# Linear attention with ReLU features: K and V with four heads on 128 partitions, a wider block-diagonal V, and the DMAs at both ends rearranged

## The chip, the cores and the metric

The kernel runs on one core of one Trainium2 chip. The metric is device time in microseconds (us). The profiler's span, from the first to the last instruction, is about 2 us shorter. PE is TensorE (matmuls), PEld its weight loads, DVE is VectorE, ACT is ScalarE, POOL is GpSimd, SP is SyncE. A name with a q (ACTq, SPq) is that engine's sequencer. "Granted clock" (PEclk) is the TensorE clock that the throttle let through, as a share of full speed.

## The reference

Eight batches of twelve heads, sequence 512, head size 64, all fp32:

```python
Q_feat = np.maximum(0, Q);  K_feat = np.maximum(0, K)          # [8, 12, 512, 64]
KV          = np.einsum('bhkd,bhkv->bhdv', K_feat, V)
K_sum       = np.sum(K_feat, axis=2)
numerator   = np.einsum('bhqd,bhdv->bhqv', Q_feat, KV)
denominator = np.einsum('bhqd,bhd->bhq', Q_feat, K_sum)
return numerator / (denominator[:, :, :, None] + 1e-10)
```

So 37.7 MB are read and 12.6 MB are written, with little arithmetic on them.

## The kernel before

The 96 heads are done in 24 groups of four. K and V of a group lie as two pairs: a pair's two heads fill 128 partitions, 64 each, so a row is 2 KB in fp32. GpSimd issues the loads and casts to bf16 on the way. V is spread into a block-diagonal tile (two heads, each with a column of ones for the K sum), so that one matmul serves two heads.

```python
def prep(g):
    kf[g] = kfp.tile([P, PR, R, 2, D], bf16, name="kf")
    nc.vector.tensor_scalar(kf[g]..., k_sb[g]..., scalar1=0.0, scalar2=None, op0=Alu.max)
    for h in range(2):                                   # V into the block diagonal, both on DVE
        hs = slice(64 * h, 64 * h + 64)
        nc.vector.tensor_copy(vbd[g % NB][hs, :, :, h, 0:D]..., v_sb[g][hs]...)

def mm_kv(g):                                            # 2 x 8 matmuls of 130 columns
    ...
def evac_kv(g):                                          # ACT, PSUM -> SBUF
    for t in range(2):
        nc.scalar.copy(kvd[...], ps_kv[g][...])
...                                                      # cut: transp, evac_qt, mm_out, norm

zero(0); prep(0)
for g in range(NG):
    mm_kv(g)
    evac_kv(g)
    if g + 1 < NG:
        ...                                              # cut: zero(g + 1) for the first groups
        prep(g + 1)
    if g > 0:
        mm_out(g - 1)
        store(g - 1, norm(g - 1))                        # SP; the last five wait for the last Q load
    transp(g)
    evac_qt(g)                                           # ACT
mm_out(NG - 1)
store(NG - 1, norm(NG - 1))
```

The order is the program's: every engine runs its share in the order in which it is written here.

Of the kernel before, what the change touches and what calls it, by code (L numbers as in the profile page):

```python
# [9 lines left out]
@with_exitstack  # L10
def kernel(
    ctx: ExitStack,
    tc: tile.TileContext,
    Q: bass.AP,
    K: bass.AP,
    V: bass.AP,
    out: bass.AP,
):
    nc = tc.nc
    B, H, S, D = Q.shape  # L20
    assert D == 64
    P = 128
    D1 = D + 1
    NH = B * H


    R = S * 2 // P
    RQ = S * 4 // P
    PR = 2
    NHG = 2 * PR  # L30
    U = RQ // 2
    NG = NH // NHG
    assert NG * NHG == NH and R == 8 and RQ == 16
    HOLD = 5

    fp32 = mybir.dt.float32
    bf16 = mybir.dt.bfloat16
    Act = mybir.ActivationFunctionType
    Alu = mybir.AluOpType

    def pool(name, bufs, **kw):
        return ctx.enter_context(tc.tile_pool(name=name, bufs=bufs, **kw))

    consts = pool("consts", 1)
    qin = pool("qin", NG)
    kin = pool("kin", 20)
    vin = pool("vin", 20)
    kfp = pool("kfp", 3)
    qtp = pool("qtp", 3)
    rcp = pool("rcp", 4)  # L50
    outp = pool("outp", 10)
    pkv = pool("pkv", 2, space=bass.MemoryType.PSUM)
    pqt = pool("pqt", 2, space=bass.MemoryType.PSUM)
    pou = pool("pou", 2, space=bass.MemoryType.PSUM)

    def rview(X):
        return X.rearrange("b h s d -> (b h s d)").rearrange(
            "(n j p f) -> n p j f", p=P, f=R * D, j=PR)

    def qview(X):  # L60
        return X.rearrange("b h s d -> (b h s d)").rearrange("(n p f) -> n p f", p=P, f=RQ * D)

    Qr, Kr, Vr, Or = qview(Q), rview(K), rview(V), qview(out)

    ident = consts.tile([P, P], bf16, name="ident")
    NB = 3



    vbf = [consts.tile([P, PR * R * 2 * D1], bf16, name=f"vbd{i}") for i in range(NB)]  # L70
    kvf = [consts.tile([P, PR * 2 * 2 * D1], bf16, name=f"kvd{i}") for i in range(NB)]
    vbd = [x.rearrange("p (j r h d) -> p j r h d", j=PR, r=R, h=2) for x in vbf]
    kvd = [x.rearrange("p (j h t d) -> p j h t d", j=PR, h=2, t=2) for x in kvf]

    ctx.enter_context(tc.manual_schedule())

    q_sb, k_sb, v_sb = {}, {}, {}
    last_q = {}

    def load(g):  # L80
        k_sb[g] = kin.tile([P, PR, R, D], bf16, name="k_sb")
        nc.gpsimd.dma_start(out=k_sb[g].rearrange("p j r d -> p j (r d)"), in_=Kr[g])  # L82
        v_sb[g] = vin.tile([P, PR, R, D], bf16, name="v_sb")
        nc.gpsimd.dma_start(out=v_sb[g].rearrange("p j r d -> p j (r d)"), in_=Vr[g])  # L84
        q_sb[g] = qin.tile([P, U, 2 * D], bf16, name="q_sb")
        last_q[g] = nc.gpsimd.dma_start(out=q_sb[g].rearrange("p u f -> p (u f)"), in_=Qr[g])  # L86

    load(0)
    make_identity(nc, ident)
    for g in range(1, NG):  # L90
        load(g)

    def zero(i):
        nc.vector.memset(vbf[i].bitcast(fp32), 0.0)  # L94
        for h in range(2):
            nc.vector.memset(vbd[i][64 * h:64 * h + 64, :, :, h, D:D1].rearrange("p j r o -> p (j r) o"), 1.0)  # L96
        nc.vector.memset(kvf[i].bitcast(fp32), 0.0)  # L97

    kf, qt, ps_kv, ps_qt, ps_out = {}, {}, {}, {}, {}

    def prep(g):
        kf[g] = kfp.tile([P, PR, R, 2, D], bf16, name="kf")
        nc.vector.tensor_scalar(  # L103
            kf[g].rearrange("p j r c d -> p (j r) c d"),
            k_sb[g].rearrange("p j r d -> p (j r) d").unsqueeze(2).to_broadcast([P, PR * R, 2, D]),
            scalar1=0.0, scalar2=None, op0=Alu.max)
        for h in range(2):
            hs = slice(64 * h, 64 * h + 64)
            nc.vector.tensor_copy(  # L109
                vbd[g % NB][hs, :, :, h, 0:D].rearrange("p j r d -> p (j r) d"),  # L110
                v_sb[g][hs].rearrange("p j r d -> p (j r) d"))

    def mm_kv(g):
        ps_kv[g] = pkv.tile([P, PR, 2, D1], fp32, name="ps_kv")
        for j in range(PR):
            for r in range(R):
                nc.tensor.matmul(  # L117
                    ps_kv[g][:, j, :, :],
                    kf[g][:, j, r, :, :].rearrange("p c d -> p (c d)"),
                    vbd[g % NB][:, j, r, :, :],  # L120
                    start=(r == 0), stop=(r == R - 1), skip_group_check=True)

    def evac_kv(g):
        for t in range(2):
            ts_ = slice(64 * t, 64 * t + 64)
            nc.scalar.copy(kvd[g % NB][ts_, :, :, t, :].rearrange("p j h d -> p (j h) d"),  # L126
                           ps_kv[g][ts_].rearrange("p j h d -> p (j h) d"))

    def transp(g):
        ps_qt[g] = pqt.tile([P, U, P], bf16, name="ps_qt")  # L130
        for u in range(U):
            nc.tensor.transpose(ps_qt[g][:, u, :], q_sb[g][:, u, :], ident)  # L132

    def evac_qt(g):
        qt[g] = qtp.tile([P, U, P], bf16, name="qt")
        nc.scalar.activation(  # L136
            qt[g].rearrange("p u q -> p (u q)"), ps_qt[g].rearrange("p u q -> p (u q)"), Act.Relu)

    def mm_out(g):
        for j in range(2):  # L140
            po = pou.tile([P, 2, 512], fp32, name="ps_out")
            ps_out[g, j] = po
            for v in range(U // 2):
                u = j * (U // 2) + v
                for h in range(NHG):
                    hs = slice(32 * h, 32 * h + 32)
                    nc.tensor.matmul(  # L147
                        po[hs, v // 2, (v % 2) * 2 * D1:(v % 2) * 2 * D1 + 2 * D1],
                        qt[g][:, u, hs],
                        kvd[g % NB][:, h // 2, h % 2, :, :],  # L150
                        start=True, stop=True, skip_group_check=True)

    def norm(g):
        o_sb = outp.tile([P, RQ, D], fp32, name="o_sb")
        for j in range(2):
            pv = ps_out[g, j][:, :, 0:4 * D1].rearrange("p b (r d) -> p b r d", d=D1)
            den = rcp.tile([P, 2, 4], fp32, name="den")
            nc.vector.tensor_scalar(den, pv[:, :, :, D], scalar1=1e-10, scalar2=None, op0=Alu.add)  # L158
            rec = rcp.tile([P, 2, 4], fp32, name="rec")
            nc.vector.reciprocal(rec, den)  # L160
            nc.vector.tensor_tensor(  # L161
                o_sb[:, 8 * j:8 * j + 8].rearrange("p (b r) d -> p b r d", b=2),
                pv[:, :, :, 0:D],
                rec.unsqueeze(3).to_broadcast([P, 2, 4, D]), op=Alu.mult)
        return o_sb

    def store(g, o_sb):
        st = nc.sync.dma_start(out=Or[g], in_=o_sb.rearrange("p r d -> p (r d)"))
        if g >= NG - HOLD:
            tc.add_manual_dep(  # L170
                st.ins, trigger.name,
                mybir.DependencyInfo(mybir.DependencyClass.Sync, mybir.DependencyReason.DATA),
                reason="the last stores follow the loads")

    trigger = last_q[NG - 1].ins

    zero(0)
    prep(0)
# [4 lines that stand above are left out]
            if g + 1 < NB:  # L183
                zero(g + 1)
# [3 lines that stand above are left out]
            store(g - 1, norm(g - 1))  # L188
        transp(g)
        evac_qt(g)  # L190
    mm_out(NG - 1)
    store(NG - 1, norm(NG - 1))


# [28 lines left out]
```

## Time and profile before

| | before |
|---|---|
| time, median of 6 runs | 136.01 us (135.62 to 136.78) |
| span of the profiled run | 133.8 us |
| one group, in the middle | 5.13 us |
| busy: PE, DVE, ACT | 76.6, 89.4, 43.8 us |

The page of the kernel before. The rows of digits cut the span into 40 slices and give the busy share in tenths; the last line is the chain of work that ended last, by engine.

```profile
span 133.8 us, 3247 instructions
PE 76.6 (57%) x1344; PEld 63.5 (47%) x1344; DVE 89.4 (67%) x228; ACT 43.8 (33%) x73; POOL 50.4 (38%) x78
...
PEclk9999999555865896896797797797556985556995
DMA  1999999999999999999999999999999999994873
...
DMA 84%; DVE 6%; issue 3%; POOL 2%; PE 1%; ACT 1%; ACTq 0%; POOLq 0%
```

The DMA engines are full from the second slice to the 36th, and the chain is 84% DMA: the kernel waits for its data. The timeline of PE in the middle (start, duration, what, and in brackets the idle time before it and what ended it):

```profile
62.19 1.89 PE L117 MATMUL ps_kv<-vbd,kf 128*128 128x130 bf16 x16 [1.97 <-DVE vbd L109]
64.02 1.06 PE L147 MATMUL ps_out<-kvd,qt 128*32 128x130 bf16 x32
...
67.32 1.10 PE L117 MATMUL ps_kv<-vbd,kf 128*128 128x130 bf16 x16 [1.69 <-DVE vbd L109]
```

K^T·V groups (ps_kv) start 5.13 us apart. In that time 1.57 MB are loaded and 0.52 MB stored: 409 GB/s. The same 16 matmuls take 1.89 us in one group and 1.10 in the next: the clock changes between half and full. Two lines of the costliest groups of instructions (after the bar: busy us in all, mean ns of one, then idle before it):

```profile
L136 ACT ACTIVATE qt<-ps_qt 128x1024 bf16<-128x1024 bf16 x24 | 24.6, 1023 | 26.7 <-PE ps_qt L132 26.7
L109 DVE COPY vbd<-v_sb 64x1024 bf16<-64x1024 bf16 x48 | 20.4, 424 | 16.9 <-DMA v_sb<-in_V_dram 16.6
```

For 1024 elements per partition ACT needs 1.02 us and DVE, copying V, 0.42. Last, the end of the kernel in stretches of 2 us (start:end, length, busy us of five engines with their instruction counts, granted clock, DMA share, GB/s):

```profile
118.00:120.00 2.00, 0.58 (x6) 0.68 (x7) 1.38 (x5) 0.55 (x1) 0.00 (x0) 0.50 1.21 204
120.00:122.00 2.00, 2.00 (x45) 1.78 (x42) 1.93 (x5) 0.57 (x2) 0.00 (x0) 0.50 0.91 161
122.00:124.00 2.00, 1.93 (x33) 1.61 (x26) 1.71 (x6) 0.89 (x2) 0.00 (x0) 0.76 0.15 31
124.00:126.00 2.00, 1.31 (x43) 0.88 (x40) 1.86 (x7) 1.05 (x3) 0.00 (x0) 1.00 0.80 324
```

(A DMA share over 1 means that packets overlap. A load counts with the bf16 bytes that it writes, half of what it reads.) From 122 to 124 us nearly nothing moves: the last five stores are held until the last Q load has landed.

### The profile page before, as it was taken

To read this page: it belongs to the slowest core of one execution; us is meant where nothing else is said; L and a number is where in the kernel's file an instruction comes from. 1 tells how busy PE (TensorE), PEld (TensorE's weight loads), DVE (VectorE), ACT (ScalarE), POOL (GpSimd) and SP (SyncE) were. 2 spreads that over 40 slices of the span, in tenths; PEclk is the share of its full clock that TensorE was granted. 3 is DMA by queue.
4 is the path that set the end of the run, shared out by engine and by line. 5 is a ranking of instruction groups with operands and counts; after the bars stand their busy time and mean duration, and the time that the engine had idled before them with its cause. 6 is when DMAs were issued, how large, how long until landed. Compare 5 with 4: busy or idle time off the path is not lost.

```text
span 133.8 us, 3247 instructions
## 1 busy us (share of the span) xinstructions
PE 76.6 (57%) x1344; PEld 63.5 (47%) x1344; DVE 89.4 (67%) x228; ACT 43.8 (33%) x73; POOL 50.4 (38%) x78
## 2 busy tenths in 40 slices
PE   0056975287485474574664654753966655949510
PEld 0056864276365455454453543642855444838410
DVE  4267886558577577577577577585685775578970
ACT  1205453133323522523523523433234333233510
POOL 6977564234334325335235244243343340000000
PEclk9999999555865896896797797797556985556995
DMA  1999999999999999999999999999999999994873
GB/s 12 180 187 206 207 207 234 284 226 279 218 271 258 228 285 249 236 283 241 247 282 232 257 281 224 265 279 217 273 259 228 283 265 224 280 207 89 322 305 157
DMA packets 19982, 31.66 MB, mean 237 GB/s; under 512 B 1536, under 2 KB 13824, under 8 KB 19968
## 3 DMA queue, kind: packets, MB, share of 16 engines
q0 software_dynamic: 16512, 18.88, 82.9%
q1 hardware_dynamic: 3456, 12.58, 24.8%
q8 instruction: 10, 0.16, 0.4%
q14 instruction: 4, 0.03, 0.1%
HBM read 37.75 MB, written 12.58 MB: 376 GB/s over the span
## 4 chain that ended last, share of the span: by engine, by line
DMA 84%; DVE 6%; issue 3%; POOL 2%; PE 1%; ACT 1%; ACTq 0%; POOLq 0%
DMA v_sb<-in_V_dram 46%; DMA q_sb<-in_Q_dram 21%; DMA k_sb<-in_K_dram 18%; DVE o_sb L161 3%; DVE vbd L109 2%; POOL k_sb L82 1%; DVE rec L160 1%; ACT qt L136 1%; DVE den L158 1%; PE ps_out L147 1%; POOL q_sb L86 0%; PE ps_qt L132 0%; POOL ident masks.py:199 0%; POOL ident masks.py:197 0%; POOL v_sb L84 0%
## 5 line engine op out<-in xcount | busy, mean ns | idle before, releaser
L117 PE MATMUL ps_kv<-vbd,kf 128*128 128x130 bf16 x384 | 37.4, 273 | 44.0 <-DVE vbd L109 43.9
L117 PEld LDWEIGHTS <-kf 128*128 128x128 bf16 x384 | 34.1, 125 | 46.6 <-issue 32.6
L126 ACT CAST kvd<-ps_kv 64x260 bf16<-64x260 f32 x48 | 17.9, 374 | 54.3 <-PE ps_kv L117 53.5
L161 DVE TENSOR_TENSOR o_sb<-ps_out,rec 128x512 f32<-128x512 f32 x48 | 33.2, 692 | 1.7
L136 ACT ACTIVATE qt<-ps_qt 128x1024 bf16<-128x1024 bf16 x24 | 24.6, 1023 | 26.7 <-PE ps_qt L132 26.7
L109 DVE COPY vbd<-v_sb 64x1024 bf16<-64x1024 bf16 x48 | 20.4, 424 | 16.9 <-DMA v_sb<-in_V_dram 16.6
L103 DVE TENSOR_SCALAR kf<-k_sb 128x2048 bf16<-128x2048 bf16 x24 | 16.7, 695 | 16.8 <-DMA k_sb<-in_K_dram 16.8
L86 POOL DMA_DIRECT2D q_sb<-in_Q_dram x24 | 15.0, 625 | 34.1 <-DMA k_sb<-in_K_dram 30.9
L147 PE MATMUL ps_out<-kvd,qt 128*32 128x130 bf16 x768 | 23.2, 274 | 7.7 <-DVE o_sb L161 4.9
L82 POOL DMA_DIRECT2D k_sb<-in_K_dram x24 | 17.7, 739 | 18.4 <-DMA v_sb<-in_V_dram 17.6
L147 PEld LDWEIGHTS <-qt 128*32 128x32 bf16 x768 | 15.6, 117 | 14.3 <-DVE o_sb L161 7.2
L84 POOL DMA_DIRECT2D v_sb<-in_V_dram x24 | 17.2, 715 | 10.7 <-DMA q_sb<-in_Q_dram 8.3
L132 PE MATMUL ps_qt<-ident,q_sb 128*128 128x128 bf16 x192 | 18.7, 256 | 0.0
L132 PEld LDWEIGHTS <-q_sb 128*128 128x128 bf16 x192 | 14.0, 115 | 3.7 <-issue 2.7
L160 DVE RECIPROCAL rec<-den 128x8 f32<-128x8 f32 x48 | 9.8, 203 | 1.6
L158 DVE TENSOR_SCALAR den<-ps_out 128x8 f32<-128x8 f32 x48 | 7.7, 161 | 1.3 <-PE ps_out L147 0.6
L94 DVE MEMSET vbd<- 128x1040 f32 x3 | 2.8, 925 | 1.6 <-PEq L207 1.0
L126 ACT ACT_TABLE_LOAD x1 | 1.3, 1283 | 2.8 <-DVE kvd L97 2.8
L97 DVE MEMSET kvd<- 128x260 f32 x3 | 0.8, 275 | 0.3
L96 DVE MEMSET vbd<- 64x16 bf16 x6 | 0.4, 72 | 0.6
masks.py:199 POOL TENSOR_SCALAR_AFFINE_SELECT ident<-ident 128x128 bf16<-128x128 bf16 x1 | 0.3, 287 | 0.1
masks.py:197 POOL MEMSET ident<- 128x128 bf16 x1 | 0.2, 243 | 0.0
(4 smaller groups left out, 0.4 us busy)
## 6 DMA issues: line engine op xcount, KB each, us to landing
out_dram<-o_sb SPq DMA_DIRECT2D x24, 512.0 KB, 6.2
k_sb<-in_K_dram POOLq DMA_DIRECT2D x24, 256.0 KB, 13.8
v_sb<-in_V_dram POOLq DMA_DIRECT2D x24, 256.0 KB, 13.9
q_sb<-in_Q_dram POOLq DMA_DIRECT2D x24, 256.0 KB, 12.5
```

The costliest lines, as they stand in the source:

```text
L82: nc.gpsimd.dma_start(out=k_sb[g].rearrange("p j r d -> p j (r d)"), in_=Kr[g])
L84: nc.gpsimd.dma_start(out=v_sb[g].rearrange("p j r d -> p j (r d)"), in_=Vr[g])
L86: last_q[g] = nc.gpsimd.dma_start(out=q_sb[g].rearrange("p u f -> p (u f)"), in_=Qr[g])
L103: nc.vector.tensor_scalar(kf[g].rearrange("p j r c d -> p (j r) c d"), k_sb[g].rearrange("p j r d -> p (j r) d").unsqueeze(2).to_broadcast ...
L109: nc.vector.tensor_copy(vbd[g % NB][hs, :, :, h, 0:D].rearrange("p j r d -> p (j r) d"), v_sb[g][hs].rearrange("p j r d -> p (j r) d"))
L117: nc.tensor.matmul(ps_kv[g][:, j, :, :], kf[g][:, j, r, :, :].rearrange("p c d -> p (c d)"), vbd[g % NB][:, j, r, :, :], start=(r == 0), s ...
L126: nc.scalar.copy(kvd[g % NB][ts_, :, :, t, :].rearrange("p j h d -> p (j h) d"), ps_kv[g][ts_].rearrange("p j h d -> p (j h) d"))
L132: nc.tensor.transpose(ps_qt[g][:, u, :], q_sb[g][:, u, :], ident)
L136: nc.scalar.activation(qt[g].rearrange("p u q -> p (u q)"), ps_qt[g].rearrange("p u q -> p (u q)"), Act.Relu)
L147: nc.tensor.matmul(po[hs, v // 2, (v % 2) * 2 * D1:(v % 2) * 2 * D1 + 2 * D1], qt[g][:, u, hs], kvd[g % NB][:, h // 2, h % 2, :, :], start ...
L160: nc.vector.reciprocal(rec, den)
L161: nc.vector.tensor_tensor(o_sb[:, 8 * j:8 * j + 8].rearrange("p (b r) d -> p b r d", b=2), pv[:, :, :, 0:D], rec.unsqueeze(3).to_broadcast ...
```

## The change

Its intent is to feed the DMA engines better: 4 KB rows for K and V as well, data flowing earlier, and no idle stretch at the end. With four heads on 128 partitions, 32 each, V's block diagonal is four heads wide, so K^T·V becomes 16 matmuls of 260 columns instead of 16 of 130. The spreading of V takes four copies of 32 partitions instead of two of 64, and two of them go to ACT.

```diff
-    R = S * 2 // P                     # K, V: two heads on 128 partitions, rows of 2 KB
-    PR = 2
+    NHG = 4
+    R = S * NHG // P                   # four heads, rows of 4 KB
...
-    load(0)
+    k_sb[0] = outp.tile([P, R, D], fp32, name="k_first", tag="o_sb")
+    nc.sync.dma_start(out=k_sb[0].rearrange("p r d -> p (r d)"), in_=Kr[0])
+    v_sb[0] = outp.tile([P, R, D], fp32, name="v_first", tag="o_sb")
+    nc.scalar.dma_start(out=v_sb[0].rearrange("p r d -> p (r d)"), in_=Vr[0])
+    load_q(0)
...                                     # cut: the K, V of the last two groups go ahead of their Q
     def prep(g):
...
-        for h in range(2):
-            hs = slice(64 * h, 64 * h + 64)
-            nc.vector.tensor_copy(...)
+        for h in range(NHG):
+            hs = slice(32 * h, 32 * h + 32)
+            dst, src = vbd[g % NB][hs, :, h, 0:D], v_sb[g][hs]
+            if h < 2:
+                nc.vector.tensor_copy(dst, src)
+            else:
+                nc.scalar.copy(dst, src)
...
     def store(g, o_sb):
-        st = nc.sync.dma_start(...)    # the last five wait for the last Q load
-        ...
+        if NG - 2 - HELD <= g < NG - 2:          # groups 17 to 21, behind the loads
+            nc.gpsimd.dma_start(out=Or[g], in_=o_sb.rearrange("p r d -> p (r d)"))
+        elif g == NG - 1:
+            ...                                  # the last store in two halves, by SP
+        else:
+            nc.sync.dma_start(...)
```

(Cut to its core, with comments added. The rest follows from the shapes, and K and V have 14 buffers instead of 20. The loop over the groups is unchanged.)

More of the change, by code (lines that the diff above doesn't have):

```diff
@@ L24 @@
     NH = B * H
-    R = S * 2 // P
-    RQ = S * 4 // P
-    PR = 2
-    NHG = 2 * PR
-    U = RQ // 2
+    NHG = 4
+    R = S * NHG // P
+    U = R // 2
     NG = NH // NHG
-    assert NG * NHG == NH and R == 8 and RQ == 16
-    HOLD = 5
+    assert NG * NHG == NH and R == 16
+    HELD = 5
     fp32 = mybir.dt.float32
@@ L45 @@
     qin = pool("qin", NG)
-    kin = pool("kin", 20)
-    vin = pool("vin", 20)
+    kin = pool("kin", 14)
+    vin = pool("vin", 14)
     kfp = pool("kfp", 3)
@@ L56, in rview @@
     def rview(X):
-        return X.rearrange("b h s d -> (b h s d)").rearrange(
-            "(n j p f) -> n p j f", p=P, f=R * D, j=PR)
-    def qview(X):
-        return X.rearrange("b h s d -> (b h s d)").rearrange("(n p f) -> n p f", p=P, f=RQ * D)
-    Qr, Kr, Vr, Or = qview(Q), rview(K), rview(V), qview(out)
+        return X.rearrange("b h s d -> (b h s d)").rearrange("(n p f) -> n p f", p=P, f=R * D)
+    Qr, Kr, Vr, Or = rview(Q), rview(K), rview(V), rview(out)
     ident = consts.tile([P, P], bf16, name="ident")
@@ L66 @@
     NB = 3
-    vbf = [consts.tile([P, PR * R * 2 * D1], bf16, name=f"vbd{i}") for i in range(NB)]
-    kvf = [consts.tile([P, PR * 2 * 2 * D1], bf16, name=f"kvd{i}") for i in range(NB)]
-    vbd = [x.rearrange("p (j r h d) -> p j r h d", j=PR, r=R, h=2) for x in vbf]
-    kvd = [x.rearrange("p (j h t d) -> p j h t d", j=PR, h=2, t=2) for x in kvf]
+    vbf = [consts.tile([P, R * NHG * D1], bf16, name=f"vbd{i}") for i in range(NB)]
+    kvf = [consts.tile([P, NHG * 2 * D1], bf16, name=f"kvd{i}") for i in range(NB)]
@@ L75 @@
+    vbd = [x.rearrange("p (r h d) -> p r h d", r=R, h=NHG) for x in vbf]
+    kvd = [x.rearrange("p (h t d) -> p h t d", h=NHG, t=2) for x in kvf]
     ctx.enter_context(tc.manual_schedule())
     q_sb, k_sb, v_sb = {}, {}, {}
-    last_q = {}
-    def load(g):
-        k_sb[g] = kin.tile([P, PR, R, D], bf16, name="k_sb")
-        nc.gpsimd.dma_start(out=k_sb[g].rearrange("p j r d -> p j (r d)"), in_=Kr[g])
-        v_sb[g] = vin.tile([P, PR, R, D], bf16, name="v_sb")
-        nc.gpsimd.dma_start(out=v_sb[g].rearrange("p j r d -> p j (r d)"), in_=Vr[g])
-        q_sb[g] = qin.tile([P, U, 2 * D], bf16, name="q_sb")
-        last_q[g] = nc.gpsimd.dma_start(out=q_sb[g].rearrange("p u f -> p (u f)"), in_=Qr[g])
@@ L88, with load_kv, load_q @@
-    load(0)
-    make_identity(nc, ident)
-    for g in range(1, NG):
-        load(g)
+    def load_kv(g):
+        k_sb[g] = kin.tile([P, R, D], bf16, name="k_sb")
+        nc.gpsimd.dma_start(out=k_sb[g].rearrange("p r d -> p (r d)"), in_=Kr[g])
+        v_sb[g] = vin.tile([P, R, D], bf16, name="v_sb")
+        nc.gpsimd.dma_start(out=v_sb[g].rearrange("p r d -> p (r d)"), in_=Vr[g])
+    def load_q(g):
+        q_sb[g] = qin.tile([P, U, 2 * D], bf16, name="q_sb")
+        nc.gpsimd.dma_start(out=q_sb[g].rearrange("p u f -> p (u f)"), in_=Qr[g])
@@ L93, in zero @@
+    k_sb[0] = outp.tile([P, R, D], fp32, name="k_first", tag="o_sb")
[3 more added lines that the diff above has]
+    load_q(0)
+    make_identity(nc, ident)
+    for g in range(1, NG - 2):
+        load_kv(g)
+        load_q(g)
+    load_kv(NG - 2)
+    load_kv(NG - 1)
+    load_q(NG - 2)
+    load_q(NG - 1)
     def zero(i):
@@ L94, in zero @@
         nc.vector.memset(vbf[i].bitcast(fp32), 0.0)
-        for h in range(2):
-            nc.vector.memset(vbd[i][64 * h:64 * h + 64, :, :, h, D:D1].rearrange("p j r o -> p (j r) o"), 1.0)
+        for h in range(NHG):
+            nc.vector.memset(vbd[i][32 * h:32 * h + 32, :, h, D:D1], 1.0)
         nc.vector.memset(kvf[i].bitcast(fp32), 0.0)
@@ L101, in prep @@
     def prep(g):
-        kf[g] = kfp.tile([P, PR, R, 2, D], bf16, name="kf")
+        kf[g] = kfp.tile([P, R, 2, D], bf16, name="kf")
         nc.vector.tensor_scalar(
-            kf[g].rearrange("p j r c d -> p (j r) c d"),
-            k_sb[g].rearrange("p j r d -> p (j r) d").unsqueeze(2).to_broadcast([P, PR * R, 2, D]),
+            kf[g], k_sb[g].unsqueeze(2).to_broadcast([P, R, 2, D]),
             scalar1=0.0, scalar2=None, op0=Alu.max)
-        for h in range(2):
-            hs = slice(64 * h, 64 * h + 64)
-            nc.vector.tensor_copy(
-                vbd[g % NB][hs, :, :, h, 0:D].rearrange("p j r d -> p (j r) d"),
-                v_sb[g][hs].rearrange("p j r d -> p (j r) d"))
-    def mm_kv(g):
-        ps_kv[g] = pkv.tile([P, PR, 2, D1], fp32, name="ps_kv")
-        for j in range(PR):
-            for r in range(R):
-                nc.tensor.matmul(
-                    ps_kv[g][:, j, :, :],
-                    kf[g][:, j, r, :, :].rearrange("p c d -> p (c d)"),
-                    vbd[g % NB][:, j, r, :, :],
-                    start=(r == 0), stop=(r == R - 1), skip_group_check=True)
+        for h in range(NHG):
+            hs = slice(32 * h, 32 * h + 32)
[4 more added lines that the diff above has]
+                nc.scalar.copy(dst, src)
+    def mm_kv(g):
+        ps_kv[g] = pkv.tile([P, NHG, D1], fp32, name="ps_kv")
+        for r in range(R):
+            nc.tensor.matmul(
+                ps_kv[g],
+                kf[g][:, r, :, :].rearrange("p c d -> p (c d)"),
+                vbd[g % NB][:, r, :, :],
+                start=(r == 0), stop=(r == R - 1), skip_group_check=True)
     def evac_kv(g):
@@ L125, in evac_kv @@
             ts_ = slice(64 * t, 64 * t + 64)
-            nc.scalar.copy(kvd[g % NB][ts_, :, :, t, :].rearrange("p j h d -> p (j h) d"),
-                           ps_kv[g][ts_].rearrange("p j h d -> p (j h) d"))
+            nc.scalar.copy(kvd[g % NB][ts_, :, t, :], ps_kv[g][ts_])
     def transp(g):
@@ L149, in mm_out @@
                         qt[g][:, u, hs],
-                        kvd[g % NB][:, h // 2, h % 2, :, :],
+                        kvd[g % NB][:, h, :, :],
                         start=True, stop=True, skip_group_check=True)
     def norm(g):
-        o_sb = outp.tile([P, RQ, D], fp32, name="o_sb")
+        o_sb = outp.tile([P, R, D], fp32, name="o_sb", tag="o_sb")
         for j in range(2):
@@ L167, in store @@
     def store(g, o_sb):
-        st = nc.sync.dma_start(out=Or[g], in_=o_sb.rearrange("p r d -> p (r d)"))
-        if g >= NG - HOLD:
-            tc.add_manual_dep(
-                st.ins, trigger.name,
-                mybir.DependencyInfo(mybir.DependencyClass.Sync, mybir.DependencyReason.DATA),
-                reason="the last stores follow the loads")
-    trigger = last_q[NG - 1].ins
+        if NG - 2 - HELD <= g < NG - 2:
+            nc.gpsimd.dma_start(out=Or[g], in_=o_sb.rearrange("p r d -> p (r d)"))
+        elif g == NG - 1:
+            for j in range(2):
+                rs = slice(R // 2 * j, R // 2 * (j + 1))
+                nc.sync.dma_start(out=Or[g].rearrange("p (r d) -> p r d", d=D)[:, rs],
+                                  in_=o_sb[:, rs])
+        else:
+            nc.sync.dma_start(out=Or[g], in_=o_sb.rearrange("p r d -> p (r d)"))
     zero(0)
```

## The prediction

> **What bounds the kernel now.** The DMA engines. The 40-slice view has their busy share at 9 tenths from 7 to 120 us; the chain of waits is 84% DMA, nearly all loads. In the timeline the K^T·V matmul groups start every 5.13 us from 42 to 93 us. One step moves 1.57 MB of loads and 0.52 MB of store: 2.10 MB / 5.13 us = 409 GB/s. Loads alone (10 to 20 us) run at about 412, stores alone (126 to 128 us) at 410, so little rate is left to win. Outside that lie 3.2 us before data flows, some 2 us at 122 to 124 us with almost no traffic (held stores wait for the last Q), and 3.5 us from the last normalization to the end.
>
> **What the change does.**
> 1. 2 KB reads become 4 KB. DMA packets take 98 ns (2 KB read) and 173 ns (4 KB), overlapping. Estimate: 0 to 0.12 us per step. The Trainium skill (DMA: Bandwidth & Descriptors, Why small descriptors are slow) gives about 3 cycles per packet, so little at 2 KB; no run separates it yet.
> 2. First K, V in fp32 by SP and ACT: data about 1.3 us earlier. Stores behind loads: removes most of the 2 us hole. DMA alone would allow a span of about 127 us.
> 3. V becomes four heads wide: the 16 K^T·V matmuls stream 260 columns instead of 130. They take 1.10 us at full clock and 1.89 at half (timeline). Estimate: 1.96 and 3.63 us.
> 4. Four V copies of 32 partitions, each still 1024 elements: two on DVE (424 ns, as now), two on ACT. ACT's 1024-element activation takes 1.02 us, so about +2.1 us per step; ACT busy rises from 44 to about 93 us.
>
> **What becomes critical.** In ACT's program order the eviction of KV(g) stands before the V copies of g+1, and K^T·V(g+1) needs those copies. So there is a loop that data cannot shorten: matmuls 1.96 + eviction 0.80 + V copies 2.10 + hand-overs 0.15 = about 5.0 us (6.7 at half clock), as long as the DMA step it replaces. The clock should stay full: in this trace it fell after windows of about 3.4 us whose PE streamed under about 36%, and held at 38% and more; the loop leaves about 43%.
>
> The loop also bites at the start, where the old kernel ran steps of 3.6 to 3.8 us. I expect K^T·V(0) at about 8 us (8.24 now), (1) at 14.5 (12.0), (2) at 21 (15.8), the PE being still at half clock; then 21 steps of 5.0 give (23) at about 126 (123.3 now). The tail stays near 10 us. Span about 136, time 2 us more. The DMA gains disappear behind this loop.
>
> **Prediction: 137.5 us, 8 in 10 between 133 and 142.** Faster by over 2%: 0.15; within 2%: 0.43; slower by over 2%: 0.42.
>
> **What would show it.** K^T·V spacing of 4.9 to 5.1 us from the third group on, not following the landings; ACT busy near 93 us, V copies near 1.02 us each; the matmul group's wait ended by ACT's V copies; PE clock close to 1.0 after 20 us; DMA share below 9 tenths in the last 15 us; ACT and PE, not DMA, most of the chain.
>
> **What would make it wrong.** ACT copies from SBUF much under 1 us: then DMA bounds again, at about 129 to 131. Half-clock windows recurring: each costs about 1.7 us, time above 140. A slow first preparation from fp32 moves everything by 1 to 2 us.

## The result

| | before | changed |
|---|---|---|
| time, median of 6 runs | 136.01 us | 149.81 us (146.57 to 152.46) |
| fast runs alone, changed over before | | 1.0846 (95% interval 1.0733 to 1.0959) |
| span, clock of the profiled run | 133.8 us, 0.781 | 148.8 us, 0.861 |
| K^T·V of group 0, 1, 2, 3, 23 starts at | 8.24, 12.01, 15.79, 19.60, 123.26 | 9.25, 15.47, 21.99, 28.57, 137.36 |

A ratio is the mean time of one kernel's fast runs over that of the other's of the same rounds, so it is not quite the ratio of the medians. Only two of the six runs of the changed kernel count as fast (146.57 and 148.76 us, granted clock 0.893 and 0.879); the others spread above them without a gap, and the profiled one, at 150.64, is among them. The three runs above 150 us have clocks of 0.861 to 0.868, the three below 149 of 0.879 to 0.893, so the spread goes with the loss of clock. Executions over 1.5% slower than the fastest of the same kernel are left out of the means.

The page of the changed kernel, the same lines:

```profile
span 148.8 us, 3341 instructions
PE 92.0 (62%) x1344; PEld 68.3 (46%) x1344; DVE 89.8 (60%) x234; ACT 94.6 (64%) x121; POOL 43.2 (29%) x81
...
PEclk9999595869996895999869789995986977999595
DMA  4999999999999999999999999999999621312333
...
ACT 35%; PE 30%; DMA 26%; issue 3%; DVE 1%; POOL 0%; ACTq 0%; POOLq 0%
```

The chain has changed hands: ACT and PE instead of DMA. The DMA engines are full only to the 31st slice, about 115 us, and the rest of the time they wait for results to store. The data side did improve: the first data packet starts at 1.8 us instead of 2.8, and from 30 to 90 us the packets carry 412 to 413 GB/s instead of 406 to 407 (summed from the packet records, loads at the size that they read). V's copies as a group, and the timeline of ACT and PE in the middle:

```profile
L116 ACT COPY vbd<-v_sb 32x1024 bf16<-32x1024 bf16 x46 | 48.6, 1057 | 1.1
L114 DVE COPY vbd<-v_sb 32x1024 bf16<-32x1024 bf16 x46 | 19.3, 419 | 0.3
```

```profile
67.23 1.95 PE L121 MATMUL ps_kv<-vbd,kf 128*128 128x260 bf16 x16 [1.96 <-ACT vbd L116]
69.11 0.64 PE L150 MATMUL ps_out<-kvd,qt 128*32 128x130 bf16 x32
69.28 0.77 ACT L130 CAST kvd<-ps_kv 64x260 bf16<-64x260 f32 x2 [1.04 <-PE ps_kv L121]
69.69 0.62 PE L135 MATMUL ps_qt<-ident,q_sb 128*128 128x128 bf16 x8
70.08 2.14 ACT L116 COPY vbd<-v_sb 32x1024 bf16<-32x1024 bf16 x2
72.24 1.02 ACT L139 ACTIVATE qt<-ps_qt 128x1024 bf16<-128x1024 bf16 x1
72.27 2.67 PE L121 MATMUL ps_kv<-vbd,kf 128*128 128x260 bf16 x16 [1.96 <-ACT vbd L116]
...
78.02 1.95 PE L121 MATMUL ps_kv<-vbd,kf 128*128 128x260 bf16 x16 [1.14 <-ACT vbd L116]
```

Read it as a ring. The matmuls end at 69.18; ACT then evicts KV (0.77) and only after that copies V for the next group (2.14); when the copies end, at 72.22, the next matmuls start. That is 5.04 us by these lines (5.03 unrounded), with no DMA in it. The next turn takes 5.75 us, because its matmuls take 2.67 instead of 1.95: part of them ran at half clock. Of the 23 turns 12 took 5.02 or 5.03 us; the other 11 took 5.55 to 6.57 and cost 12.4 us together (128.1 us from the first K^T·V to the last, less 23 times 5.03).

The clock is granted in windows of 3.41 us. Four neighbouring ones of the changed kernel, cut at those windows' borders, with the columns as above:

```profile
66.51:69.92 3.41, 2.69 (x53) 2.16 (x52) 1.86 (x6) 2.32 (x4) 1.06 (x2) 1.00 1.11 251
69.92:73.34 3.42, 1.46 (x17) 1.20 (x15) 3.06 (x8) 3.27 (x4) 0.53 (x1) 1.00 1.09 282
73.34:76.75 3.41, 3.41 (x48) 2.45 (x47) 1.13 (x4) 1.67 (x3) 1.59 (x3) 0.50 1.11 255
76.75:80.16 3.41, 2.27 (x38) 1.72 (x39) 2.24 (x5) 2.32 (x4) 1.06 (x2) 1.00 1.10 237
```

In the second window PE is busy for 1.46 of 3.42 us, because the gap before K^T·V falls into it, and the next window is at half clock. In that one PE is busy all the time, and the clock comes back.

### The profile page after: what moved, and what is told of

The parts are those of the page before. It is cut to its first block, busy times and chain, and to the rows that moved or that the text cites. A ratio compares the mean times of both kernels' runs of the same rounds, so it can differ in the third digit from the quotient of the medians.

```text
span 148.8 us, 3341 instructions
## 1 busy us (share of the span) xinstructions
PE 92.0 (62%) x1344; PEld 68.3 (46%) x1344; DVE 89.8 (60%) x234; ACT 94.6 (64%) x121; POOL 43.2 (29%) x81
## 4 chain that ended last, share of the span: by engine, by line
ACT 35%; PE 30%; DMA 26%; issue 3%; DVE 1%; POOL 0%; ACTq 0%; POOLq 0%
PE ps_kv L121 29%; ACT vbd L116 26%; DMA k_sb<-in_K_dram 11%; ACT kvd L130 9%; DMA v_sb<-in_V_dram 8%; DMA q_sb<-in_Q_dram 7%; PE ps_out L150 1%; DVE o_sb L164 1%; ACT qt L139 1%; PE ps_qt L135 0%; DVE rec L163 0%; ACTq L130 0%; DVE den L161 0%; POOL ident masks.py:199 0%; POOL ident masks.py:197 0%
## 5 line engine op out<-in xcount | busy, mean ns | idle before, releaser
L121 PE MATMUL ps_kv<-vbd,kf 128*128 128x260 bf16 x384 | 60.4, 323 | 50.7 <-ACT vbd L116 50.7
L121 PEld LDWEIGHTS <-kf 128*128 128x128 bf16 x384 | 43.3, 113 | 63.9 <-issue 44.8
L116 ACT COPY vbd<-v_sb 32x1024 bf16<-32x1024 bf16 x46 | 48.6, 1057 | 1.1
L139 ACT ACTIVATE qt<-ps_qt 128x1024 bf16<-128x1024 bf16 x24 | 24.6, 1025 | 1.5 <-PE ps_qt L135 0.9
L74 POOL DMA_DIRECT2D k_sb<-in_K_dram x23 | 13.4, 582 | 22.1 <-DMA v_sb<-in_V_dram 14.8
L114 DVE COPY vbd<-v_sb 32x1024 bf16<-32x1024 bf16 x46 | 19.3, 419 | 0.3
L150 PE MATMUL ps_out<-kvd,qt 128*32 128x130 bf16 x768 | 18.4, 250 | 1.2 <-ACT qt L139 1.2
L76 POOL DMA_DIRECT2D v_sb<-in_V_dram x23 | 12.5, 542 | 20.6 <-DMA q_sb<-in_Q_dram 13.5
L135 PE MATMUL ps_qt<-ident,q_sb 128*128 128x128 bf16 x192 | 16.5, 235 | 0.0
L174 POOL DMA_DIRECT2D out_dram<-o_sb x5 | 3.6, 710 | 29.3 <-DVE o_sb L164 29.3
L98 DVE MEMSET vbd<- 128x2080 f32 x3 | 5.4, 1792 | 2.2 <-PEq L213 1.2
L116 ACT ACT_TABLE_LOAD x1 | 1.3, 1283 | 5.8 <-DMA v_first<-in_V_dram 5.8
```

The costliest lines, as they stand in the source:

```text
L74: nc.gpsimd.dma_start(out=k_sb[g].rearrange("p r d -> p (r d)"), in_=Kr[g])
L76: nc.gpsimd.dma_start(out=v_sb[g].rearrange("p r d -> p (r d)"), in_=Vr[g])
L114: nc.vector.tensor_copy(dst, src)
L116: nc.scalar.copy(dst, src)
L121: nc.tensor.matmul(ps_kv[g], kf[g][:, r, :, :].rearrange("p c d -> p (c d)"), vbd[g % NB][:, r, :, :], start=(r == 0), stop=(r == R - 1), ...
L135: nc.tensor.transpose(ps_qt[g][:, u, :], q_sb[g][:, u, :], ident)
```

## The experiments

Two theories of the loss have to be told apart from each other and from simpler ones. The loop: ACT's order of work ties the matmuls of one group to those of the next. The clock: the loop's gap makes PE lose its full clock again and again. Rivals: ACT simply has too much work, or PE has.

### 1. V copies ahead of the eviction (e1_copies_first)

```diff
     for g in range(NG):
         mm_kv(g)
-        evac_kv(g)
         if g + 1 < NG:
             ...
             prep(g + 1)
+        evac_kv(g)
```

Expected:

> The change with one thing moved: on ACT the two V copies of group g+1 stand before the eviction of KV(g). Theory A (the loop matmuls, eviction, V copies, matmuls is what bounds the changed kernel): the loop is gone, K^T.V spacing falls to the DMA's step of about 5.07 us (2.10 MB at 413 GB/s), DMA share 9 tenths to near the end, time 129 to 132 us, although ACT still does 94 us of work. Rival B (ACT is simply too busy with the V copies, or its copies slow the others): ACT's work is unchanged, so the time stays above 140 us.

Measured: 131.17 us (131.11 to 131.23), 0.9639 of before (0.9586 to 0.9692). In its page ACT's busy time is the same 94.6 us, and DMA is back as the chain:

```profile
PE 87.0 (67%) x1344; PEld 66.1 (51%) x1344; DVE 92.6 (72%) x234; ACT 94.6 (73%) x121; POOL 43.5 (34%) x81
...
PEclk9999999999959999599689779869859959999996
DMA  3999999999999999999999999999999999999844
...
DMA 83%; ACT 5%; issue 3%; PE 3%; DVE 2%; POOL 1%; POOLq 0%; ACTq 0%
```

Moving one call, with the same work on every engine, takes about 16 us off (1.0846 less 0.9639, times 136; 18.6 by the medians). The loop is what bounded the changed kernel; ACT's amount of work was not. PE's timeline in the middle is worth a look:

```profile
61.65 3.02 PE L121 MATMUL ps_kv<-vbd,kf 128*128 128x260 bf16 x16 [2.00 <-ACT vbd L116]
...
66.72 1.95 PE L121 MATMUL ps_kv<-vbd,kf 128*128 128x260 bf16 x16 [0.46 <-ACT vbd L116]
...
71.79 2.93 PE L121 MATMUL ps_kv<-vbd,kf 128*128 128x260 bf16 x16 [2.00 <-ACT vbd L116]
```

The clock still falls (3.02 and 2.93 against 1.95), but the groups keep their 5.07 us: a slow group only shortens the idle time before the next one, 0.46 instead of 2.00. Half clock cost nothing here, where PE's matmuls are not in the loop.

### 2. All V copies on DVE (e2_all_dve)

```diff
-            if h < 2:
+            if h < 4:
                 nc.vector.tensor_copy(dst, src)
```

Expected:

> The change with all four V copies on DVE, none on ACT. Theory A (loop through ACT): the loop is gone; DVE has 4 x 0.42 + 0.69 + 2.1 = about 4.5 us per step, under the DMA's 5.07, so the time falls to 129 to 134 us. Rival C (the wider matmuls themselves, 260 columns at a clock that falls to half, are too slow whatever ACT does): PE's work is unchanged, so the time stays above 140 us.

Measured: 131.71 us (131.61 to 132.0), ratio 0.9682; DVE was busy for 111.3 us (85%), ACT for 43.9. Cutting the loop at the other end does nearly as well. The wider matmuls are the same here and in the first experiment, so they alone are no obstacle.

### 3. The loop kept, PE's gap filled (e3_fill_pe)

```diff
+        for rep in range(3):
             for u in range(U):
                 nc.tensor.transpose(ps_qt[g][:, u, :], q_sb[g][:, u, :], ident)
```

Expected:

> The change with every Q transpose written three times into the same place (same result), so that the gap in PE's stream before the next K^T.V group shrinks from 2.1 us to about 1.2; the loop through ACT is untouched. Theory A2 (the predicted loop of 5.03 us is right, and the rest of the loss is half-clock windows set off by that gap): no half-clock window after the start, spacing 5.03 us from about the third group to the last, time 138 to 140 us, some 10 us less than the changed kernel, though PE does more work. Rival C (PE has too much work): more PE work makes it slower, over 150 us.

Measured: 138.95 us (138.75 to 139.11), ratio 1.021 (1.0153 to 1.0267), granted clock 0.995. More work on PE made the changed kernel about 9 us faster (means of the fast runs, each against before in its own rounds: 1.0846 less 1.021, times 136; as the changed kernel has only two fast runs, its interval alone leaves this open by 1.5 us either way). The page with its chain, and windows at the borders of this trace's own grid of 3.41 us:

```profile
PEclk9999999999999999999999999999999999999997
DMA  4999999999999999999999999999999999950334
...
ACT 50%; PE 37%; issue 5%; DMA 4%; DVE 2%; ACTq 0%
...
67.56:70.98 3.42, 2.47 (x61) 2.01 (x59) 2.43 (x7) 2.80 (x4) 1.59 (x3) 1.00 1.10 264
70.98:74.39 3.41, 3.29 (x63) 2.76 (x63) 1.83 (x6) 2.30 (x5) 1.36 (x3) 1.00 1.11 238
74.39:77.80 3.41, 2.35 (x28) 2.00 (x25) 2.51 (x7) 2.68 (x3) 1.13 (x3) 1.00 1.09 271
```

From 16 to 129 us no window falls below 2.3 us of busy PE, and no clock is lost after the start until the last matmuls are done. From the second group on, every turn takes 4.97 to 5.03 us, to the end. So the loss splits: about 9 us of it came from the half clock, and the rest of the distance to experiment 1, about 8 us (138.95 less 131.17), is the loop at full clock. These 8 us do not come from the middle: there a turn of 5.03 us is no longer than experiment 1's 5.07, which the DMA sets. They come from the two ends, where few or no stores run beside the loads and experiment 1 takes mostly 3.6 to 4.5 us a group: its K^T·V(0) to (6) take 26.5 us against 31.7 here, the last three turns 12.1 against 15.1.

### 4. How much filling is enough (f_fill1, f_fill4)

For a finer measure than "busy", which counts the modelled tail of each burst, I took 0.165 us of tail off each matmul record of the trace, joined what was left, and call that streaming. (At full clock a transpose's record lasts 0.220 us, and the next starts after 0.056.) In the traces of before and of the change, a full-clock window with a streaming share of 0.367 or less was always followed by half clock, and one of 0.381 or more never. These two kernels write one and four of the eight transposes twice.

```diff
-        for u in range(U):
+        for u in list(range(U)) + list(range(1)):        # f_fill4: range(4)
             nc.tensor.transpose(ps_qt[g][:, u, :], q_sb[g][:, u, :], ident)
```

Expected, one and four:

> The change with one of the eight Q transposes of each group written twice (0.056 us more PE streaming per step; result unchanged). Theory A2 with a threshold: over both traces a full-clock window of 3.4 us was followed by half clock when PE streamed 0.367 of it or less, and stayed at full clock from 0.381 on; the changed kernel's low windows stand at 0.34 to 0.37. One more transpose adds 0.016, so most of the low windows stay under: half-clock windows still recur, 144 to 150 us. Rival: if the clock answers to the share of time in general, rather than to a threshold, nothing much changes either, but then four more won't change much.

> The same with four of the eight transposes written twice (0.22 us more PE streaming per step). Theory A2 with a threshold: the low windows rise by 0.065 to 0.40 and more, above 0.381, so no half-clock window after the start: 138 to 140 us, as with all transposes tripled. Rival (a gradual effect): between, 143 to 147 us.

Measured: 146.62 us (144.86 to 151.54) with one, 140.89 (140.01 to 142.78) with four; granted clock in the profiled runs 0.937 (a slow run, 147.8 us) and 0.972. With one, the median is as expected. With four it was not quite: all four runs lie above 138 to 140 us, the median by 1 us, and in the profiled one, the fastest, a half-clock window was left in the loop, after one that streamed 0.380. With one, a window of 0.374 fell and one of 0.375 held. Over the traces of the eleven different kernels full clock was lost after 0.380 at most and kept from 0.370 on. The twelfth trace, the repeat of experiment 1, is wider: windows of 0.387 and 0.391 lost it and one of 0.368 kept it. So the border lies at 0.37 to 0.39, about as finely as this reading of the records can tell. (If the windows are cut 0.05 us earlier than recorded, all twelve traces agree on 0.380 lost and 0.382 kept; but this shift was sought afterwards, and no run tests it.) It speaks for a border and against a gradual effect: 0.22 us of extra PE work per group brings about four fifths of what 0.9 us brings (1.0846 less 1.0323, against 1.0846 less 1.021).

### 5. The DMA side alone (e4_before_dma)

The kernel before, with its compute and its 2 KB rows, and with the first K and V by SP and ACT, the order of the last loads, the stores behind the loads and the 14 buffers of the change.

```diff
-    load(0)
+    k_sb[0] = outp.tile([P, PR, R, D], fp32, name="k_first", tag="o_sb")
+    nc.sync.dma_start(out=k_sb[0].rearrange("p j r d -> p j (r d)"), in_=Kr[0])
+    ...                              # V by ACT; last K and V ahead of the last Q; store() of the change
```

Expected:

> The kernel before with only the DMA side of the change: first K and V in fp32 by SP and ACT, the last K and V ahead of the last Q, stores of five groups behind the loads on the GpSimd queue, the last store in halves, 14 buffers; K and V still two heads on 128 partitions (2 KB rows), compute as before. Theory: data start 1 us earlier and the idle stretch near 122 us goes: 130 to 133 us, 3 to 5 us less than before, rate in the middle still 406 GB/s. If the DMA parts are worth nothing, 135 to 137 us.

Measured: 131.62 us (131.36 to 131.94), ratio 0.9666 (0.9601 to 0.9731), 406 to 407 GB/s between 30 and 90 us. The two ends are worth about 4.5 us by themselves. Experiment 1, with 4 KB rows, carries 412 GB/s there, yet is only 0.45 us faster, and the intervals of the two ratios overlap.

### 6. Looking for a still better version (b1_tail, b2_tail_split, b3_split)

In experiment 1 the last groups follow each other in 4.0 us, while the loads without stores bring a group every 3.8; ACT is full there (1.93 of 2 us). b1_tail moved part of the last groups' work ahead of the last K^T·V, b2_tail_split also gave DVE a third V copy in odd groups:

```diff
+    transp(NG - 1)
+    evac_qt(NG - 1)
+    mm_out(NG - 2)
+    store(NG - 2, norm(NG - 2))
     mm_kv(NG - 1)
...
-            if h < 2:                    # b2_tail_split only
+            if h < 2 + g % 2:
```

> For a version that beats both: copies first as in the first experiment, and for the last group only, its transposes, its Q eviction and the products and normalization of the group before moved ahead of its K^T.V. After K^T.V(23) only eviction, products, normalization and store are left, about 1.5 us less than now: 129.3 to 130.3 us against 131.2. If the end is set by the stores still queued instead, no change: 131 us.

> The same, and every second group has three V copies on DVE and one on ACT (ACT 3.4 us, DVE 3.85 us per step on average instead of 4.0 and 3.65). In the last stretch, where only loads flow and a group's data comes every 3.8 us, the steps were 4.0 us long because ACT was full; they should fall to about 3.85: 0.3 to 0.8 us under the version without. If DVE's longer row makes the end later, none or slower by up to 0.5.

Measured: 132.39 us (132.07 to 133.56) and 131.91 (130.91 to 132.21). The first expectation failed. The second version is 0.5 us under the first, as expected of it, but not for the reason given: its steps in the last stretch, 4.17 and 4.06 us, did not fall to 3.85. Neither beats experiment 1. PE takes its instructions in order, and the products of group 22 need a Q eviction that ACT does only after the V copies of group 23; K^T·V(23) stood behind them and started at 122.15 us in b1_tail, against 119.41 in experiment 1.

b3_split drops that and keeps the uneven split, run beside a repeat of experiment 1:

```diff
-            if h < 2:
+            if h < (4 if g == NG - 1 else 2 + g % 2):
```

> The same kernel as the first experiment, run again so that the next one is compared with it on one chip: 131.0 to 131.5 us.

> For a version that beats both, with the mistake of the tail versions undone: PE's order is that of the first experiment (there, moving the products of group 22 ahead of K^T.V(23) made PE wait for a Q eviction that ACT does only after its V copies; K^T.V(23) began at 122.2 us instead of 119.4). Copies first; odd groups with three V copies on DVE and one on ACT, the last group with all four on DVE. K^T.V(23) should begin at 118 to 119 us, and the time be 129.8 to 130.8 us, 0.4 to 1.4 less than copies first alone. If only the stores at the end or DVE set the end, 131 us or more.

Measured: 131.26 us (131.09 to 131.55) for the repeat and 131.01 (130.68 to 131.67) for b3_split, ratios 0.9638 and 0.9624 with intervals that overlap almost entirely. The 129.8 to 130.8 expected of b3_split were missed: no gain that can be told from none. Now DVE is nearly full at the end (1.94 and 1.84 of 2 us from 116 to 120 us) and K^T·V(23) starts at 119.27. By the rates, 4 KB rows should give 1.8 us (50.3 MB at 407 and at 413 GB/s); where all but half a microsecond of it goes is not settled, beyond that the last groups wait for ACT or DVE rather than for data. The version to keep is experiment 1, 131.2 us: it beats both kernels.

## Why the prediction was wrong

Predicted were 137.5 us, within 133 and 142; measured, 149.81.

- **What bounds the kernel before, and how little rate there is to win: right.** The middle rate rose by 1.5%.
- **DMA gains at the ends: right.** Experiment 5 shows them alone, about 4.5 us.
- **The loop through ACT: right, in kind and in size.** Predicted were matmuls of 1.96 us, copies of 2.10, an ACT busy for 93 us and about 5.0 us per turn. Measured: 1.95, 2.14, 94.6 and 5.03. Experiments 1 and 2 show that taking the loop away takes its cost away.
- **The start: nearly right.** K^T·V(0), (1), (2) were foreseen at 8, 14.5 and 21 us and came at 9.25, 15.47 and 21.99. ACT put its table load (1.28 us) behind the wait for the first V, which I had not looked for.
- **"The clock should stay full" is the step that failed**, and with it "then 21 steps of 5.0". The clock granted was 0.861 on average, with half clock in 9 of these 21 turns. From the third group to the last took 115.4 us instead of 105. Of the 12.8 us between the span foreseen (136) and measured (148.8), these steps are 10.4; 1.0 came from the start and 1.4 from the tail, whose last matmuls also ran partly at half clock. (These are figures of the profiled run; the fastest, at a clock of 0.893, has a span of 144.8 and no trace.) With the clock held full, in experiment 3, the changed kernel takes 138.95 us, well inside the range.

The mistake in that step can be named. The border itself, between 36% and 38%, was read correctly from the trace before, and it held in the other traces but for the repeat of experiment 1, which strays by about 0.01. But "the loop leaves about 43%" was worked out from the recorded lengths of the bursts, tails included (the record does not hold the working, but the measured figures below fit it), while the border had been read in streaming time, tails taken off. In recorded busy time the low window of the changed kernel is indeed 1.46 of 3.42 us, or 43%; in streaming time it is 0.366, which is under the border. Two measures were compared as if they were one. Windows of the kernel before, cut at its own borders, would have warned: there 1.41 us of recorded busy time lost the clock, and 1.72 kept it, so 1.46 was on the wrong side or close to it.

```profile
58.12:61.53 3.41, 1.41 (x41) 1.04 (x41) 1.96 (x6) 1.77 (x3) 0.79 (x2) 1.00 1.13 259
61.53:64.95 3.42, 2.76 (x48) 2.39 (x47) 2.63 (x8) 0.75 (x2) 1.46 (x2) 0.50 1.16 281
64.95:68.36 3.41, 1.72 (x32) 1.46 (x24) 2.53 (x7) 1.02 (x2) 1.77 (x3) 1.00 1.19 225
68.36:71.77 3.41, 1.43 (x41) 1.04 (x41) 1.97 (x6) 1.77 (x3) 0.81 (x2) 1.00 1.13 261
```

The prediction did name this as what could break it: "Half-clock windows recurring: each costs about 1.7 us, time above 140." Measured, a turn with half clock in it costs 1.1 us on average (12.4 us over 11 turns); the time given for it was right, its chance was put too low.

## What to carry to other kernels

When work moves to an engine that is half idle, look at where it stands in that engine's order: behind an instruction that waits for this step's result, it ties the next step to this one, and then durations add up that used to overlap. Here the same 94.6 us of ACT work stayed hidden in one order and cost some 16 us in another, about 9 of them through the half clock. If a step sits on a margin (here the TensorE clock's), measure the margin and the step with the same ruler, and give the other side of it a fair chance in the range.

## What the Trainium skill lacked or had wrong

- **TensorE: Matmul & The Clock Gate** (HAM oscillation): its rule of thumb is to leave no PE-idle gap above about 3.4 us. Here idle gaps of 1.96 us were enough to lose the full clock, over and over. What decided was how much of a 3.41 us window PE streamed: in the traces of the eleven kernels full clock was lost after windows of 0.380 at most and kept after windows of 0.370 and more (with the repeat of experiment 1: 0.391 and 0.368). From half clock, full came back after 0.755 and more, and not after 0.722 and less. The page gives no such share.
- **TensorE: Matmul & The Clock Gate** (HAM oscillation): its remedies for the clock are another loop order, or padding M to 512 and more. Padding too is work of no other use; a smaller dose of it is to repeat matmuls inside the gap. Tripled transposes made the changed kernel some 9 us faster, although in a kernel whose loop is the real fault. The transposes must count as activity here: without them ten windows of experiment 3 would stream only 0.19 to 0.32, under the border, and full clock held.
- **ScalarE: Activation LUTs** (What ACT_TABLE_LOAD costs): it states 186 ns + 0.833 ns per element, and an overlap of 93 ns for back-to-back ACTIVATEs. The 1024-element ACTIVATE took 1025 ns, and ACT's COPYs of that size 1057 ns on average (the formula gives 1039). Where two ACTIVATEs follow each other (b1_tail and b2_tail_split) they overlap by 103 ns, so the page is right. COPYs do not overlap: a pair took 2.14 us, with 24 ns between the two records. The page does not give this difference. Its 1283 ns for a table load is what was measured.
- **DMA: Bandwidth & Descriptors** (Why small descriptors are slow): the 3 cycles per packet give an estimate of 1.1% for K and V, half of the bytes, going from 64 to 128 beats of 32 bytes. Measured were 406 to 407 and 412 to 413 GB/s, 1.5%. The page has no measurement on trn2 of 2 KB against 4 KB rows in HBM.
